# Modulation products and sums of squares issued four at a time, one per column group of TensorE

## The chip, the cores and the metric

The kernel is one program on one core of a Trainium2 chip. The metric is device time in microseconds, the median of several runs of the same program. A core has five engines that run their own instruction streams: TensorE (PE in the profile, with its weight loads shown apart as PEld), VectorE (DVE), ScalarE (ACT), GpSimd (POOL) and SyncE (SP), which issues the DMA transfers. They meet through semaphores.

## The reference

The model is a two-layer backbone for a flow-matching network: 1024 latent tokens with a prefix of 256 context tokens, 1024 features, all in float32. Both layers have the same frame, of which the change touches two parts:

```
def rms_norm(x, g):
    y = x * lax.rsqrt(jnp.mean(x * x, axis=-1, keepdims=True) + EPS)
    return y * g

def ada_mod(cond, w, b):
    m = (silu(cond) @ w + b)          # [1024] @ [1024, 6144]
    return jnp.split(m, 6, axis=-1)   # shift, scale, gate, twice

x = x + gate1 * mixer(rms_norm(x, g1) * (1 + scale1) + shift1)
x = x + gate2 * conv_ffn(rms_norm(x, g2) * (1 + scale2) + shift2)
```

Latent tokens are modulated with the conditioning `c` and context tokens with `c_ctx`. Layer 0's mixer is a gated MLP beside a bidirectional gated DeltaNet; layer 1's mixer is a latent attention of 8 heads. The ConvFFN is a projection up to 5632 features, a depthwise convolution of width 3, `silu(g) * u`, and a projection down. A last RMS norm ends the model.

## The kernel before, in words

Features lie on the 128 partitions, tokens along the free axis. A value of 1024 features is eight tiles `k`, and the tokens are cut into chunks of 256 or 512. Each float32 product of the model's large matrices is made of three float32r passes over halves of the operands (`mm3`, lines 146 to 148: high by high, high by low, low by high), which are 128 columns wide on TensorE. The order of the work on each engine is set by two things: the program's text, in which generators are woven into one another (`weave`, `chain`, `par`: a step of a norm after each step of a product), and then the compiler's scheduler, which moves instructions by its own estimate of when their operands are there.

Two kinds of product are narrow, in full float32, with 32 columns of weights, and their results lie in one of four groups of 32 partitions of a PSUM bank, a column group of TensorE each (`tile_position=(0, 32 * q)`).

*The modulation* (`ada`, line 251). A unit is 512 output features; a layer has 12 units. The weight matrix of a unit comes in four tiles `adaw` of 128 by 1024 elements (512 KB, line 271): tile `k2` holds two `k` tiles of 512 features. When a tile is there, two products are issued (line 281), each over 512 columns, on column groups 0 and 1 or 2 and 3; `start` is set for the first four `k`, `stop` for the last four. After the fourth tile ACT copies the bank to `adam` (line 285), TensorE transposes it in four products (`adat`, line 260) and DVE sums the four groups (line 262). Units 0 to 11 of layer 0 are made before and beside the first mixer's projections; those of layer 1 are made beside layer 0's ConvFFN, one step of the generator after each product group of `up` (`pump`, in `ffn`).

*The norms* (`rnorm`, line 189). For each of the eight tiles a square is made, two of three on ACT (line 203) and one of three on POOL (line 201), and right behind each square comes one product with a matrix of ones (line 205), 256 or 512 columns, on column group `k % 4`. DVE copies the four partial sums (line 208), one more product adds them up and spreads them over the partitions (`nall`, line 211), and DVE and ACT make the reciprocal root (`rsqrt`, line 217). `mod_h` (line 232) then makes the halves `hh`, `hl` of the modulated value with DVE, ACT and POOL. The rooms for squares (`sq`) and for modulated tiles (`h`) are handed out by three functions: `temps` (line 170), `borrow` (line 178) and `carve` (near line 460).

*The places.* Layer 0's second norm is woven between the last products of its output projection (`out0`, tiles `wo`) and the first of the ConvFFN (tiles `up`); the norm before layer 1 runs as a tail beside layer 0's last `down` products (tiles `dn`); layer 1's second norm runs beside the attention's output projection (`out1`); the final norm is the tail of layer 1's ConvFFN, chunk by chunk (`END`), where `ENDP` says after which products the steps of the chunk before are taken. DVE adds each `down` or `wo` result to the stream `xa` (lines 350, 1293, 1605), and DVE and POOL make the halves of every weight tile (lines 132 and 139).

Of the kernel before, what the change touches and what calls it, by code (L numbers as in the profile page):

```python
# [30 lines left out]
# chunks of the tokens (context first), and of the latent ones alone  # L31
CHN = [(0, 256), (256, 512), (768, 512)]
LAT = [(0, 512), (512, 512)]
# the chunks of the first tile and of the last products of a ConvFFN
CHB = [(0, 256), (512, 512), (256, 256), (1024, 256)]
END = [(0, 512), (512, 256), (768, 256)]
# a ConvFFN's order, by its tiles to a group (1 in layer 0, 2 in layer 1): the products after which a step of
# the norm of the chunk before comes, the product from which on the chunk's own norm steps, the steps of the
# last norms within the first tile, and the products held back for the last group
ENDP = {1: (0, 1, 3, 5), 2: (0, 2, 4, 6)}  # L40
# [3 lines left out]
# where the DVE holds the others up: every third sum for the ACT and the Pool  # L44
RELIEF = (3, 1)
# the final norm's tiles for the ACT and the Pool
POOLK = (1, 4, 7)
# GDN: the chunks in rounds of inverses, and the chunks by which the loads of these lag
ROUNDS = [[0, 1, 2, 9], [3, 8, 4, 7], [5, 6]]
LAG = 2  # L50
# gMLP: the chunks from here on stay on the chip
YD = NC - 3
# the queries' tiles: two heads' rotary parts after the first of their plain parts
# [3 lines left out]
def f(ap):  # L57
    return ap.bitcast(F32)


def bc(ap, axis, n):
    """insert a broadcast axis of n at position axis."""
    a = ap.unsqueeze(axis)
    shape = list(a.shape)
    shape[axis] = n
    return a.broadcast_to(shape)
# [8 lines left out]
def weave(main, fill, n=1, rest=True):  # L75
    """n steps of fill after each step of main, then the rest of fill."""
    for _ in main:
        for _ in range(n):
            next(fill, None)
    if rest:  # L80
        drain(fill)


def par(*gens):
    """steps of several generators at once: (generator, steps of it to a step)."""
# [19 lines left out]
class Kern:  # L105
# [4 lines left out]
    # ------------------------------------------------------------ helpers  # L110
    def act(self, out, in_, func, **kw):
        """an activation; Ln and Exp from the table set that has both."""
# [23 lines left out]
    def split(self, hi, lo, src, eng):  # L136
        """src = hi + lo exactly, each in float32r's significand."""
# [3 lines left out]
    def mm3(self, ps, ws, xs, first=True, last=True):  # L141
        """ps += sum of w.T @ x, each product in three float32r passes."""
# [7 lines left out]
    def weights(self, pool, src, shape, tag, eng, bufs_raw=2, bufs=2, n=None):  # L150
        """the halves of a weight (of the first n parts of a room)."""
# [8 lines left out]
    def stream(self, pool, srcs, shape, tag, eng, bufs_raw=2, bufs=2, n=None):  # L160
        """get(i): the halves of the i-th weight; the one after it is to be asked for while it is used."""
# [8 lines left out]
    def temps(self, pool, tag="n", nsq=3, nt=2, nr=2, width=512):  # L170
        """rooms of [P, width] for a norm: called with the temporary's name."""
        def get(name):
            t = {"m": "sq", "t": "sq", "pt": "sq"}.get(name, name)
# [4 lines left out]
    def borrow(self, rooms):  # L178
        """a norm's temporaries in ten rooms."""
        cnt = {"sq": 0, "h": 0}  # L180

        def get(name):
            if name in cnt:
                cnt[name] += 1
                return rooms[4 + cnt[name] % 3 + (3 if name == "h" else 0)]
# [3 lines left out]
    def rnorm(self, tmp, xs, cn, d, res, steps=False):  # L189
        """res: rsqrt(mean over features of x^2 + eps), the same in all partitions, [P, cn].  # L190
        Yields where the PE would wait; with steps, before each x too."""
# [3 lines left out]
        last = {i % g: i for i in range(len(xs))}  # L195
        for i, x in enumerate(xs):
            if steps:
                yield
            sq = tmp("sq")[:, :cn]
            if i % 3 == 2:  # L200
                nc.gpsimd.tensor_tensor(sq, x, x, ALU.mult)
            else:
                nc.scalar.activation(sq, x, AF.Square)
            q = i % g
            nc.tensor.matmul(ps[32 * q:32 * q + 32, :cn], self.ones[:, :32], sq, start=i < g,  # L205
                             stop=i == last[q], tile_position=(0, 32 * q), skip_group_check=True)
# [10 lines left out]
    def rsqrt(self, r, m, t):  # L217
        """r = m ** -0.5: from the tables, then one Newton step.  t is room for a temporary."""
# [7 lines left out]
    def affine(self, t, k, gs, sh, hi, lo):  # L226
        """hi + lo = t * gs + sh (t is overwritten)."""
# [1668 lines left out]
```

## Time and profile before

| what | value |
|---|---|
| median of three runs | 3355.82 us (3353.28 to 3362.9) |
| span of the profiled execution | 3355.8 us |
| PE busy | 3246.5 us (97%), 18141 matmul records |
| DVE, ACT, POOL busy | 60%, 30%, 28% |
| modulation products (line 281), PE busy | 95.2 us, 384 records |
| sums of squares (line 205), PE busy | 91 us, 348 records |

The profile gives no time of the profiled execution beside its span; the span lies within 0.1 us of the median. A full float32 product leaves two records in the trace, a float32r product one, so 384 records are 192 products. [...]

### The profile page before, as it was taken

The page shows a single profiled execution, that of the slowest core. Times are in us where ns is not written, and L with a number is a line of the kernel's source. Part 1 is how long each engine was busy: PE and PEld are TensorE (multiplying, and loading weights), DVE is VectorE, ACT ScalarE, POOL GpSimd, SP SyncE. Part 2 cuts the span into 40 slices and gives each one's busy share as a digit, 9 for nine tenths or more (in the row PEclk, how much of TensorE's full clock was granted, in tenths as well). Part 3 has the DMA queues.
Part 4 walks back from the last instruction along what each step waited for, and adds up shares of the span by engine and source line. Part 5 has one row for each costly group of instructions (what it writes and reads, how often), then busy time and mean ns, then how long its engine had stood idle before and what let it go on. Part 6 is the DMA issues. An engine that isn't in the chain of part 4 may idle for free.

```text
span 3355.8 us, 45952 instructions
## 1 busy us (share of the span) xinstructions
PE 3246.5 (97%) x18141; PEld 2623.7 (78%) x18141; DVE 1998.5 (60%) x3343; ACT 1014.4 (30%) x2116; POOL 943.1 (28%) x993
## 2 busy tenths in 40 slices
PE   7999899999999999999999999999998999999997
PEld 4667777887677877878887778988977788888885
DVE  6333876567666666666665656666656544444445
ACT  5322233333411111111113446555532211111112
POOL 4134323654311111111113332122234322212222
PEclk9999999999999999999999999999999999999999
DMA  7344946752222222221111231000032111111111
GB/s 258 108 132 126 300 137 208 230 154 85 88 70 63 73 72 70 69 76 44 38 38 44 67 102 46 26 22 21 7 132 101 57 44 57 44 44 52 49 38 50
DMA packets 199911, 289.07 MB, mean 86 GB/s; under 512 B 43776, under 2 KB 136400, under 8 KB 199568
## 3 DMA queue, kind: packets, MB, share of 16 engines
q1 hardware_dynamic: 199696, 286.14, 26.9%
q8 instruction: 143, 2.34, 0.3%
q14 instruction: 72, 0.59, 0.1%
HBM read 240.70 MB, written 45.39 MB: 85 GB/s over the span
## 4 chain that ended last, share of the span: by engine, by line
PE 69%; DVE 4%; ACT 2%; issue 1%; POOL 1%; DMA 1%; SPq 0%; DVEq 0%; POOLq 0%; ACTq 0%
PE up L146 11%; PE up L147 11%; PE up L148 11%; PE dn L146 5%; PE dn L147 5%; PE dn L148 5%; PE nsum L205 2%; PE ada L281 1%; PE pt L1532 1%; PE wo L148 1%; PE sc L1501 1%; PE wo L146 1%; PE wo L147 1%; PE o L147 1%; PE o L148 1%
## 5 line engine op out<-in xcount | busy, mean ns | idle before, releaser
L350 DVE SCALAR_TENSOR_TENSOR xa<-dn,mv,xa 128x512 f32<-128x512 f32 (+1 forms) x687 | 438.2, 670 | 402.8 <-PE dn L148 401.6
L132 POOL TENSOR_SCALAR wuh<-wur 128x1024 fp32r<-128x1024 f32 (+1 forms) x134 | 143.1, 1069 | 1108.6 <-PE up L147 1010.4
L365 ACT ACTIVATE raw<-up 128x512 f32<-128x512 f32 (+1 forms) x224 | 123.2, 550 | 1085.7 <-PE up L148 857.0
L146 PE MATMUL up<-hh,wuh 128*128 128x512 f32 (+1 forms) x1072 | 380.4, 356 | 2.1 <-ACT hh L247 1.2
L147 PE MATMUL up<-hl,wuh 128*128 128x512 f32 (+1 forms) x1072 | 377.5, 352 | 0.7 <-POOL hl L230 0.7
L148 PE MATMUL up<-hh,wul 128*128 128x512 f32 (+1 forms) x1072 | 375.9, 351 | 1.2 <-DVE wul L139 1.2
L147 PE MATMUL dn<-al,wdh 128*128 128x512 f32 (+1 forms) x880 | 323.3, 370 | 0.0
L148 PE MATMUL dn<-ah,wdl 128*128 128x512 f32 (+1 forms) x880 | 320.9, 368 | 0.0
L146 PE MATMUL dn<-ah,wdh 128*128 128x512 f32 (+1 forms) x880 | 320.5, 374 | 0.3 <-POOL wdh L132 0.3
L139 DVE TENSOR_TENSOR wul<-wur,wuh 128x1024 fp32r<-128x1024 f32 (+1 forms) x131 | 158.9, 1215 | 197.8 <-POOL wuh L132 197.3
L146 PEld LDWEIGHTS up<-hh,wuh 128*128 128x128 f32 x1072 | 201.9, 189 | 55.9 <-issue 13.4
L147 PEld LDWEIGHTS up<-hl,wuh 128*128 128x128 f32 x1072 | 202.5, 189 | 30.8 <-POOL hl L230 1.1
L148 PEld LDWEIGHTS up<-hh,wul 128*128 128x128 f32 x1072 | 202.4, 189 | 28.9 <-DVE wul L139 1.6
L146 PEld LDWEIGHTS dn<-ah,wdh 128*128 128x128 f32 x880 | 164.1, 189 | 52.6 <-issue 6.4
L148 PEld LDWEIGHTS dn<-ah,wdl 128*128 128x128 f32 x880 | 166.3, 189 | 31.3 <-issue 1.2
L147 PEld LDWEIGHTS dn<-al,wdh 128*128 128x128 f32 x880 | 166.2, 189 | 30.2 <-issue 1.7
L146 PE MATMUL proj<-hh,wih 128*128 128x512 f32 (+1 forms) x512 | 184.7, 362 | 3.4 <-POOL wih L132 3.3
L147 PE MATMUL proj<-hl,wih 128*128 128x512 f32 (+1 forms) x512 | 177.4, 347 | 1.1 <-DVE hl L248 1.1
L480 DVE SCALAR_TENSOR_TENSOR y<-raw,fconv,y 128x1023 f32<-128x1023 f32 (+1 forms) x132 | 161.1, 1221 | 28.1 <-ACT y L366 28.0
L148 PE MATMUL proj<-hh,wil 128*128 128x512 f32 (+1 forms) x512 | 176.9, 346 | 0.0
L1524 POOL TENSOR_SCALAR p<-p,rsm 128x1280 f32<-128x1280 f32 x63 | 84.5, 1341 | 325.8 <-DVE rsm L1517 164.8
L391 POOL TENSOR_TENSOR y<-y,y 128x1280 f32<-128x1280 f32 (+1 forms) x44 | 125.3, 2847 | 168.2 <-DVE y L482 160.5
(451 smaller groups left out, 7813.4 us busy)
## 6 DMA issues: line engine op xcount, KB each, us to landing
adaw<-in_ada_w SPq DMA_DIRECT2D x96, 512.0 KB, 3.6
wur<-in_w_up SPq DMA_DIRECT2D x88, 512.0 KB, 3.5
wdr<-in_w_down SPq DMA_DIRECT2D x44, 512.0 KB, 3.5
t<-t SPq DMA_DIRECT2D x20, 768.0 KB, 6.5
wur<-in_w_out SPq DMA_DIRECT2D x24, 512.0 KB, 3.3
wir<-in_w_t SPq DMA_DIRECT2D x20, 512.0 KB, 4.4
na<-na SPq DMA_DIRECT2D x10, 1024.0 KB, 8.6
t<-kq SPq DMA_DIRECT2D x8, 640.0 KB, 4.2
```

The source lines that it names most:

```text
L132: nc.gpsimd.tensor_scalar(dst, src, 1.0, 0.0, op0=ALU.mult, op1=ALU.add)
L139: (self.nc.gpsimd if eng == "pools" else self.nc.vector).tensor_tensor(lo, src, f(hi), ALU.subtract)
L146: nc.tensor.matmul(ps, wh, xh, start=first and i == 0, stop=False)
L147: nc.tensor.matmul(ps, wh, xl, start=False, stop=False)
L148: nc.tensor.matmul(ps, wl, xh, start=False, stop=last and i == n - 1)
L205: nc.tensor.matmul(ps[32 * q:32 * q + 32, :cn], self.ones[:, :32], sq, start=i < g, stop=i == last[q], tile_position=(0, 32 * q), skip_gro ...
L281: nc.tensor.matmul(ps[32 * q:32 * q + 32, :], self.cst[:, k, :], w[:, 512 * j:512 * j + 512], start=k < 4, stop=k >= 4, tile_position=(0, ...
L350: nc.vector.scalar_tensor_tensor(out=dst, in0=ps, scalar=g2[:, r, ot:ot + 1], in1=dst, op0=ALU.mult, op1=ALU.add)
L365: nc.scalar.activation(raw[:, c0:c0 + cn], ps, AF.Copy)
L391: nc.gpsimd.tensor_tensor(ys[1], ys[0], ys[1], ALU.mult)
L480: nc.vector.scalar_tensor_tensor(out=y[:, s0 + 1:e], in0=raw[:, s0:e - 1], scalar=w[:, 0:1], in1=y[:, s0 + 1:e], op0=ALU.mult, op1=ALU.add)
L1524: nc.gpsimd.tensor_scalar(p, p, rs, 0.0, op0=ALU.mult, op1=ALU.add)
```

## The change

*Modulation.* The weight matrix is laid out anew in memory: tile `k2` now holds four `k` tiles of 256 features each. Each tile thus gives four products of 256 columns, one for each column group, in place of two of 512. The number of tiles, their size and the order of their loads in the program stay. The first two tiles of a unit fill the first 256 columns of the bank, the other two the rest.

*Norms.* `rnorm` collects squares and issues the products of four together, on four column groups, instead of one behind each square. So that four squares can be held, the rooms are divided anew: in `temps` for the norms beside `out0` there are five rooms that squares and modulated tiles share (before, three and two); `borrow` has four for squares instead of three, one shared with `h`; `carve` has four instead of two, with `h` in what is left. `ENDP` for layer 1 is (0, 1, 4, 6) instead of (0, 2, 4, 6). Comments are gone too, so line numbers differ.

```diff
-ENDP = {1: (0, 1, 3, 5), 2: (0, 2, 4, 6)}
+ENDP = {1: (0, 1, 3, 5), 2: (0, 1, 4, 6)}
...
     def temps(self, pool, tag="n", nsq=3, nt=2, nr=2, width=512):
-            t = {"m": "sq", "t": "sq", "pt": "sq"}.get(name, name)
+            t = {"m": "sq", "t": "sq", "pt": "sq", "h": "h" if nt else "sq"}.get(name, name)
...
     def borrow(self, rooms):
-                return rooms[4 + cnt[name] % 3 + (3 if name == "h" else 0)]
+                return rooms[4 + cnt[name] % 4 if name == "sq" else 7 + cnt[name] % 3]
...
     def rnorm(self, tmp, xs, cn, d, res, steps=False):
+        made = []
+        def products():
+            for i, sq in made:
+                q = i % g
+                nc.tensor.matmul(ps[32 * q:32 * q + 32, :cn], self.ones[:, :32], sq, start=i < g,
+                                 stop=i == last[q], tile_position=(0, 32 * q), skip_group_check=True)
+            made.clear()
         for i, x in enumerate(xs):
-            if steps:
+            if steps and i:
                 yield
+            if len(made) == g:
+                products()
             sq = tmp("sq")[:, :cn]
...
-            q = i % g
-            nc.tensor.matmul(ps[32 * q:32 * q + 32, :cn], self.ones[:, :32], sq, start=i < g,
-                             stop=i == last[q], tile_position=(0, 32 * q), skip_group_check=True)
+            made.append((i, sq))
+        if steps:
+            yield
+        products()
...
     def ada(self, pool, tag, l, units, bufs=3, room=None, mp=None):
-                for j in range(2):
-                    k = 2 * k2 + j
-                    q = k % 4
-                    nc.tensor.matmul(ps[32 * q:32 * q + 32, :], self.cst[:, k, :], w[:, 512 * j:512 * j + 512],
-                                     start=k < 4, stop=k >= 4, tile_position=(0, 32 * q), skip_group_check=True)
+                j, kh = divmod(k2, 2)
+                for q in range(4):
+                    nc.tensor.matmul(ps[32 * q:32 * q + 32, 256 * j:256 * j + 256], self.cst[:, 4 * kh + q, :],
+                                     w[:, 256 * q:256 * q + 256], start=kh == 0, stop=kh == 1,
+                                     tile_position=(0, 32 * q), skip_group_check=True)
...
         rooms = self.carve(([f(half_a("ah")), f(half_a("al"))] if G == 1 else [room("raw"), room("raw1")])
-                           + [room("y0"), room("y1")], *([sp.tile([P, 512], F32, tag="dnt", name="dnt")] if G == 1 else []))
+                           + [room("y0"), room("y1")],
+                           sp.tile([P, 512], F32, tag="dnt", name="dnt") if G == 1 else f(half_a("ah"))[:, :512])
...
     def carve(self, rooms, *more):
-        kinds = {"sq": h[0:2], "h": h[2:4] + list(more), **{n: [r] for n, r in zip(("pt", "m", "t", "r"), h[4:])}}
+        kinds = {"sq": h[0:4], "h": list(more) or h[2:4], **{n: [r] for n, r in zip(("pt", "m", "t", "r"), h[4:])}}
+        if more:
+            kinds["h"].append(h[6])
+            kinds["t"] = kinds["pt"]
...
-                tmps = self.temps(np_, nsq=3, nr=1, nt=2, width=256)
+                tmps = self.temps(np_, nsq=5, nr=1, nt=0, width=256)
...
-    o["ada_w"] = i["ada_w"].reshape(2, KD // 2, 2, P, 12, 512).transpose(0, 4, 1, 3, 2, 5).reshape(2, 12, KD // 2, P, 1024)
+    o["ada_w"] = i["ada_w"].reshape(2, 2, 4, P, 12, 2, 256).transpose(0, 4, 5, 1, 3, 2, 6).reshape(2, 12, 4, P, 1024)
```

What the scheduler makes of it is seen in the compiled order of each engine. TensorE's stream holds the same 13104 float32r products before and after, and outside the surroundings of the norms and of the modulation they stand in the same sequence. First, TensorE in layer 0's ConvFFN, where layer 1's modulation lies between the `up` and `dn` products; before:

```order
L147 MATMUL up<-hl_7261,wuh 128x512
L148 MATMUL up<-hh_7260,wul 128x512
L281 MATMUL ada<-adaw,cst_64 32x512 x2
L146 MATMUL dn<-ah,wdh 128x256 x6
L147 MATMUL dn<-al,wdh 128x256
```

and now:

```order
L147 MATMUL up<-hl_7357,wuh 128x512
L148 MATMUL up<-hh_7356,wul 128x512
L292 MATMUL ada<-adaw,cst_64 32x256 x4
L146 MATMUL dn<-ah,wdh 128x256 x6
L147 MATMUL dn<-al,wdh 128x256
```

The place is the same, and four products of 256 columns stand where two of 512 stood. Second, TensorE beside `out0` of layer 0, where a norm of 256 tokens is woven between the `wo` products; before, within one norm:

```order
L148 MATMUL wo<-ybh_7529,wul 128x256
L146 MATMUL wo<-ybh_7529,wuh 128x256
L205 MATMUL nsum<-nsq,cst_66 32x256
L147 MATMUL wo<-ybl_7530,wuh 128x256
L148 MATMUL wo<-ybh_7529,wul 128x256
L146 MATMUL wo<-ybh_7529,wuh 128x256
L147 MATMUL wo<-ybl_7530,wuh 128x256
L148 MATMUL wo<-ybh_7529,wul 128x256
L146 MATMUL wo<-ybh_7529,wuh 128x256
L205 MATMUL nsum<-nsq,cst_66 32x256 x2
```

and now:

```order
L146 MATMUL wo<-ybh_7377,wuh 128x256
L147 MATMUL wo<-ybl_7378,wuh 128x256
L202 MATMUL nsum<-nsq,cst_66 32x256 x4
L146 MATMUL wo<-ybh_7625,wuh 128x256
L147 MATMUL wo<-ybl_7626,wuh 128x256
L202 MATMUL nsum<-nsq,cst_66 32x256
L146 MATMUL wo<-ybh_7377,wuh 128x256
```

The norm's eight products stood in six places and now stand in three: four together, then one, and the last three further on (they are not shown). The scheduler does not keep every four together. Third, DVE at the end of the program, where the final norm of the second of three chunks (512 tokens, then 256 and 256) meets the last sums of `xa`; before:

```order
L213 TENSOR_SCALAR y_27731<-nall 128x256
L350 SCALAR_TENSOR_TENSOR xa_22308<-dn,mv_13316,xa_22308 128x256 x2
L223 SCALAR_TENSOR_TENSOR y_27732<-y_27732,y_27731 128x256
L350 SCALAR_TENSOR_TENSOR xa_22308<-dn,mv_13316,xa_22308 128x256
L224 SCALAR_TENSOR_TENSOR y_27732<-y_27732 128x256
L1805 SCALAR_TENSOR_TENSOR xa_22308<-xa_22308,norm_g,y_27732 128x256 x5
L208 COPY y_27731<-nsum 128x256
```

and now:

```order
L225 TENSOR_SCALAR y_27923<-nall 128x256
L362 SCALAR_TENSOR_TENSOR xa_22500<-dn,mv_13508,xa_22500 128x256
L235 SCALAR_TENSOR_TENSOR y_27923<-y_27923 128x256
L236 SCALAR_TENSOR_TENSOR y_27924<-y_27923,y_27924 128x256
L1820 SCALAR_TENSOR_TENSOR xa_22500<-xa_22500,norm_g,y_27924 128x256 x5
L362 SCALAR_TENSOR_TENSOR xa_22500<-dn,mv_13508,xa_22500 128x256 x2
L220 COPY y_27923<-nsum 128x256
```

The last two sums of `xa` stood ahead of the five products that finish the second chunk and now stand behind them, so that the last chunk's last squares come after these. On SP the number and the sizes of the loads are the same; in the first layer's start the first projection weight `wir` is issued after eleven `adaw` tiles instead of twelve.

More of the change, by code (lines that the diff above doesn't have):

```diff
@@ L445, in ffn @@
         rooms = self.carve(([f(half_a("ah")), f(half_a("al"))] if G == 1 else [room("raw"), room("raw1")])
-                           + [room("y0"), room("y1")], *([sp.tile([P, 512], F32, tag="dnt", name="dnt")] if G == 1 else []))
+                           + [room("y0"), room("y1")], sp.tile([P, 512], F32, tag="dnt", name="dnt") if G == 1 else f(half_a("ah"))[:, :512])
         for c0, cn in ends:
```

## The prediction

> **What bounds the kernel now.** I read the page's busy times and chain first, then stretches of the span by stage, then the narrow products one by one.
>
> ```profile
> PE 3246.5 (97%) x18141; PEld 2623.7 (78%) x18141; DVE 1998.5 (60%) x3343; ACT 1014.4 (30%) x2116; POOL 943.1 (28%) x993
> PE 69%; DVE 4%; ACT 2%; issue 1%; POOL 1%; DMA 1%; SPq 0%; DVEq 0%; POOLq 0%; ACTq 0%
> ```
>
> TensorE is busy for 97% of the span and carries 69% of the chain; the next engine, DVE, carries 4%. By stage (span of the stretch, then PE, PEld, DVE, ACT, POOL busy, clock, DMA share and rate):
>
> ```profile
> 0.00:27.00 27.00, 14.51 (x76) 4.66 (x76) 7.09 (x18) 10.82 (x20) 5.14 (x11) 0.99 0.95 363
> 60.00:270.00 210.00, 200.98 (x1111) 138.39 (x1111) 80.99 (x142) 67.20 (x119) 72.79 (x86) 0.98 0.40 125
> 775.00:880.00 105.00, 101.50 (x575) 72.25 (x576) 77.23 (x136) 45.15 (x104) 40.34 (x54) 1.00 0.28 88
> 880.00:1520.00 640.00, 637.22 (x3246) 507.84 (x3247) 412.48 (x538) 117.13 (x204) 118.52 (x75) 1.00 0.21 69
> 2505.00:2600.00 95.00, 86.00 (x552) 68.17 (x552) 62.48 (x73) 23.96 (x46) 42.47 (x37) 1.00 0.29 101
> 3290.00:3356.00 66.00, 48.69 (x220) 29.41 (x218) 39.91 (x59) 18.84 (x37) 18.55 (x19) 0.91 0.18 64
> ```
>
> From 880 to 1520 us (ConvFFN of layer 0 with layer 1's modulation beside it) TensorE idles 2.8 of 640 us: what leaves its stream there leaves the time. The norms at 775 to 880 and the first projections are nearly as full. The first 27 us are loads (DMA share 0.95), and the last 66 us have TensorE at 74%: chains of the final norm decide there.
>
> **What a narrow product costs the stream.** Four places in the trace (start, duration, records):
>
> ```profile
> 1089.31 0.27 PE L148 MATMUL dn<-ah,wdl 128*128 128x256 f32 x1
> 1089.52 1.05 PE L281 MATMUL ada<-adaw,cst 128*32 128x512 f32 x4
> 1090.50 0.39 PE L146 MATMUL up<-hh,wuh 128*128 128x256 f32 x1
> 1090.72 0.28 PE L147 MATMUL up<-hl,wuh 128*128 128x256 f32 x1
> 1090.84 0.28 PE L148 MATMUL up<-hh,wul 128*128 128x256 f32 x1
> ...
> 813.84 0.28 PE L146 MATMUL wo<-ybh,wuh 128*128 128x256 f32 x1
> 814.04 0.62 PE L205 MATMUL nsum<-nsq,cst 128*32 128x256 f32 x2
> 814.59 0.38 PE L147 MATMUL wo<-ybl,wuh 128*128 128x256 f32 x1
> 814.81 0.28 PE L148 MATMUL wo<-ybh,wul 128*128 128x256 f32 x1
> ...
> 815.50 0.63 PE L205 MATMUL nsum<-nsq,cst 128*32 128x256 f32 x4
> 816.06 0.38 PE L147 MATMUL wo<-ybl,wuh 128*128 128x256 f32 x1
> ...
> 39.42 0.64 PE L205 MATMUL nsum<-nsq,cst 128*32 128x256 f32 x8
> 39.99 0.39 PE L147 MATMUL proj<-hl,wih 128*128 128x256 f32 x1
> ```
>
> Wide products of 256 columns start every 0.12 us (1090.72 to 1090.84). One sum of squares (two records) stretches 813.84 to 814.81 to 0.97 us, where two wide ones alone take 0.24: it costs 0.73. A modulation pair stretches 1089.31 to 1090.72 to 1.41 us: it costs 1.17. So a second 256 columns on the same column group costs 0.43 to 0.44 (a round, below), and about 0.31 is paid once for each place where narrow work breaks into the wide stream, split before and behind: 813.84 to 814.04 is 0.20 instead of 0.12, 814.59 to 814.81 is 0.22. Products on different groups are free beside one another: from the first narrow start to the next wide one it is 0.55 us for one product, 0.56 for two (815.50 to 816.06) and 0.57 for four (39.42 to 39.99). Thus a place costs 0.31 plus 0.43 per round of the fullest column group. A modulation tile goes from 2 rounds to 1; a norm of 256 tokens whose eight products stood alone pays 8 x 0.74 = 5.9 us, and in two fours 1.5.
>
> [...]
>
> **The change part by part.** The compiled order of TensorE gives places and rounds; times are the formula's.
>
> | stage, us | places, rounds before | now | by formula |
> |---|---|---|---|
> | 0 to 27 | 3, 14 | 3, 14 | 0.0 |
> | 27 to 270 | 35, 73 | 38, 52 | -8.1 |
> | 775 to 880 | 30, 38 | 14, 22 | -11.8 |
> | 880 to 1520 | 42, 84 | 42, 42 | -18.0 |
> | 1790 to 1962 | 34, 48 | 32, 45 | -1.9 |
> | 2505 to 2600 | 15, 22 | 11, 17 | -3.4 |
> | 3290 to end | 11, 19 | 14, 20 | +1.3 |
>
> The fours of the norms are not all kept: in layer 1 the scheduler leaves most products of 512 tokens alone, so little is won there. What each term is worth on the path:
>
> ```profile
> 880.00:1520.00 640.00, 44.19 (x168) 6.08 (x168) 1.00 0.21 69
> 800.00:820.00 20.00, 19.63 (x110) 14.61 (x109) 17.74 (x34) 8.51 (x21) 9.45 (x13) 1.00 0.20 52
> PE ada L281 <- DMA adaw<-in_ada_w: 3.2, 2, 1.8
> PE wo L148 <- DVE wul L139: 7.0, 6, 2.3
> PE nsum L205 <- ACT ah L203: 2.1, 5, 0.6
> PE nall L211 <- DVE y L208: 5.0, 2, 3.5
> ```
>
> The first row is the modulation alone: 168 records, two a product and two products a tile, are 42 tiles. 42 x 0.43 = 18.0, and I take all of it, since nothing else is near its limit: DVE is busy 412 of 640 us. From 17.0 to 18.5.
>
> 775 to 880: 11.8, but DVE was busy 17.74 of 20 us at 800 to 820. With the stretch some 2 us shorter it would be full, and its sums of `wo` then hold TensorE's banks; I take 2.5 off: 9.3 (6.5 to 11.8).
>
> 27 to 270: 8.1. TensorE waits 3.2 us here for modulation tiles (two of them, 1.8 the longest); what is won ahead of such a wait is lost at it. I take 7.0 (5.5 to 8.1). The start gains where a unit's last tile lands and its copy, transposes and the first `hh` hang on it: one round, 0.4 (0 to 0.9).
>
> 1790 to 1962: 1.9, and the 2.1 us in which a product waited for a square, because only two rooms rotated, should half go: 3.0 (0 to 4). Here modulated tiles rotate through two rooms instead of three, which is the lower end's reason.
>
> 2505 to 2600: 3.4, but TensorE waits 7.0 us for weight halves (`wul`) that come no sooner; I take 1.5 (0 to 3.4).
>
> The end: +1.3 by formula. Before, the second chunk's sums waited on DVE:
>
> ```profile
> 3328.69 6.91 DVE L1805 SCALAR_TENSOR_TENSOR xa<-xa,norm_g,y 128x512 f32<-128x512 f32 x5
> 3335.52 0.41 DVE L208 COPY y<-nsum 128x256 f32<-128x256 f32 x1
> ```
>
> That copy (and through it `nall`, which waited 5.0 us in all) still stands behind these five. The last chunk's last two sums of `xa` now stand behind the second chunk's five, which adds their 2 x 0.48 us, a square and a product of 0.7 ahead of the last copy; four square rooms take away some 2 us of waits before. I set 0 (-3 to +3).
>
> Sum: 18.0 + 9.3 + 7.0 + 0.4 + 3.0 + 1.5 + 0 = 39.2. The profiled span is 3355.8 and the median of the runs 3355.82, so no offset: **3317 us**. All ends low give 3355.8 - 26 = 3330, all high 3355.8 - 49.7 = 3306.
>
> **Rivals.**
>
> *DVE takes over beside the norms.* TensorE's stream shortens, but where norms are woven in, what feeds it sets the pace (17.74 of 20 us above; 7.0 us for `wul`). Against it: over 775 to 880 DVE has 28 us free. Then only the modulation counts, 18.0 + 7.0 + 0.4: 3330 us.
>
> *More than the stream.* With four square rooms the waits inside the norms go too: the 2.5 us taken off at 775, 2 at 1790, some 4 at the end: 3317 - 8.5 = 3308 us. For it: squares wait for products, not the reverse, where two rooms rotate; against it: the second chunk's copy remains behind DVE's five.
>
> *The groups hold TensorE up: slower.* A four cannot start before its last square, and everything wide queued behind it on TensorE waits too.
>
> ```profile
> 861.58 0.42 ACT L203 ACTIVATE ah<-xa 128x256 f32<-128x256 f32 x1 [1.03 <-PE nsum L205]
> 869.08 0.61 POOL L201 TENSOR_TENSOR ah<-xa 128x256 f32<-128x256 f32 x1 [1.33 <-PE nsum L205]
> 3308.60 0.63 ACT L203 ACTIVATE raw<-xa 128x512 f32<-128x512 f32 x1 [5.16 <-PE nsum L205]
> 3303.28 1.04 POOL L201 TENSOR_TENSOR raw<-xa 128x512 f32<-128x512 f32 x1 [7.12 <-PE nsum L205]
> ```
>
> If it stood through three squares at each of two groups of 15 norms (11 of 256 tokens: 0.42 + 0.42 + 0.61 = 1.45; 4 of 512: 2.3), that is 22 x 1.45 + 8 x 2.3 = 50 us against 39 won: 3367 us. It decides from 1.3 us a group on. Against it: the woven steps put wide products between the squares, and where fours could not be ready the scheduler split them.
>
> *Four streams slow one another.* Each reads its own moving operand, and the trace has but one clean four (0.57 us). If a four cost half a round more, 0.2 us, at some 100 fours: 3317 + 20 = 3337 us. The row itself says 0.02.
>
> [...]
>
> **How the numbers follow.** The forecast 58%, DVE takes over 18%, more than the stream 14%, four streams 5%, slower 3%, and 2% for no effect at all. The likeliest case's own range is 3306 to 3330; with most of its two neighbours 3304 to 3334. Runs of this kernel differ by up to 10 us (3353.28 to 3362.9), so 0.3% is about what can be told from no change. Faster by more than that, below 3345.7, takes in the first four cases: 95%; within it 2%; slower 3%.
>
> **What would show it.** Modulation: 42 places between 880 and 1520 us that cost 0.74 instead of 1.17, the stretch some 18 us shorter, TensorE still above 99% there. Norms: fewer places at 775 to 880 and a stretch near 96 us; if it stays above 99 with DVE above 90%, DVE took over. Fours: a first narrow start to next wide start of 0.57; 0.65 or more means the streams disturb one another. Waits of `nsum` for squares that grow past 10 us would show groups that hold TensorE up. The end: last `xa` sum to end of span. I am wrong if the modulation stretch shrinks by less than 15 us, or if attention and layer 1's ConvFFN, which the order leaves alone, move by more than 3 us each.

## The result, and the profile after

The changed kernel takes **3322.04 us** (median of four runs, 3321.32 to 3323.69) against 3356.61 us for the kernel before beside it: ratio 0.9895, 95% interval 0.9883 to 0.9906. A second set gave 3323.04 us and 0.9896 (0.9883 to 0.9910). The profiled execution's span is 3319.5 us, 36.3 less than before; 39.2 were forecast. The forecast of 3317 us was nearly right as a sum, but one of its terms came out with the wrong sign, and others made up for it. Executions whose granted clock was lower from end to end are left out of the times below; one of them is the profiled execution of the first kernel with weight halves on POOL (0.749 over the span), so its trace gives no times.

First the whole, from the page of the changed kernel: busy times, and the chain that ended last.

```profile
PE 3200.2 (96%) x18525; PEld 2628.9 (79%) x18525; DVE 1996.5 (60%) x3343; ACT 1014.0 (31%) x2116; POOL 947.8 (29%) x993
PE 68%; DVE 4%; ACT 2%; POOL 1%; issue 1%; DMA 0%; DVEq 0%; POOLq 0%; ACTq 0%; SPq 0%
```

PE lost 46 us of busy time, but the span only 36: TensorE idles 10 us more than before. Below, stretches of the span are cut at the same wide products in both kernels, so that each holds the same float32r work. The columns are length, then PE, PEld, DVE, ACT and POOL busy, the granted clock, DMA share and rate. Before:

```profile
0.00:270.08 270.08, 246.22 (x1390) 160.75 (x1391) 112.37 (x204) 99.40 (x196) 95.51 (x120) 0.98 0.50 165
775.21:880.06 104.85, 101.34 (x575) 72.10 (x575) 77.08 (x136) 45.21 (x104) 40.13 (x54) 1.00 0.28 88
880.06:1520.20 640.14, 637.36 (x3247) 507.94 (x3247) 412.42 (x538) 117.07 (x204) 118.52 (x75) 1.00 0.21 69
2505.06:2620.21 115.15, 103.93 (x650) 82.92 (x649) 77.32 (x91) 32.91 (x64) 51.44 (x46) 1.00 0.27 93
```

and after:

```profile
0.00:258.48 258.48, 233.26 (x1583) 163.61 (x1583) 112.20 (x204) 99.86 (x196) 96.51 (x120) 0.97 0.52 173
763.49:871.19 107.70, 94.92 (x601) 74.31 (x599) 76.28 (x135) 43.25 (x102) 43.06 (x54) 0.97 0.28 86
871.19:1494.06 622.87, 620.08 (x3414) 507.97 (x3414) 411.11 (x538) 117.16 (x204) 118.64 (x75) 1.00 0.22 71
2471.55:2585.33 113.78, 101.81 (x650) 84.23 (x649) 76.62 (x91) 31.87 (x63) 52.05 (x45) 0.97 0.28 93
```

The ConvFFN stretch gives 17.3 us and the first 270 give 11.6. The stretch of the norms beside layer 0's output projection (called 775 to 880 below) is the surprise: PE has 6.4 us less to do, and the stretch is 2.9 us longer.

The price of a place, from the timeline of TensorE after: start, duration, records. Records overlap (the one of 0.28 us at 803.38 is followed by a start 0.21 us later), so the price is read from the distance between starts.

```profile
942.20 0.27 PE L148 MATMUL dn<-ah,wdl 128*128 128x256 f32 x1
942.40 0.64 PE L292 MATMUL ada<-adaw,cst 128*32 128x256 f32 x8
942.97 0.39 PE L146 MATMUL up<-hh,wuh 128*128 128x256 f32 x1
943.20 0.28 PE L147 MATMUL up<-hl,wuh 128*128 128x256 f32 x1
...
802.59 0.64 PE L202 MATMUL nsum<-nsq,cst 128*32 128x256 f32 x8
803.16 0.39 PE L146 MATMUL wo<-ybh,wuh 128*128 128x256 f32 x1
803.38 0.28 PE L147 MATMUL wo<-ybl,wuh 128*128 128x256 f32 x1
803.59 0.62 PE L202 MATMUL nsum<-nsq,cst 128*32 128x256 f32 x2
804.14 0.39 PE L146 MATMUL wo<-ybh,wuh 128*128 128x256 f32 x1
```

From 942.20 to 943.20 it is 1.00 us where two wide products alone take 0.24, so a modulation tile now costs 0.76, against 1.17 before; 42 tiles at 0.41 are 17.2, and the stretch gave 17.3. A four takes 0.57 us from its first start to the next wide one (942.40 to 942.97, 802.59 to 803.16), a single product 0.55 (803.59 to 804.14): four column groups really run beside one another.

What ate the gain of the norms is seen in the waits of TensorE (waited for, us in total, times, longest). Before, 775.21 to 880.06, the first rows:

```profile
PE up L146 <- ACT hh L247: 1.2, 1, 1.2
PE wo L148 <- DVE wol L139: 0.7, 1, 0.7
PE nall L211 <- DVE npt L208: 0.7, 1, 0.7
```

After, 763.49 to 871.19:

```profile
PE nsum L202 <- ACT nsq L214: 3.9, 1, 3.9
PE wo L147 <- DVE ybl L139: 1.8, 1, 1.8
PE nsum L202 <- POOL nsq L212: 1.8, 1, 1.8
PE up L146 <- ACT hh L259: 1.7, 2, 1.2
```

and the longest of them, in the timeline of the changed kernel (the brackets: idle before, and what ended it):

```profile
822.44 0.47 DVE L260 SCALAR_TENSOR_TENSOR hl<-nh,mv,hh 128x256 fp32r<-128x256 f32 x1
822.94 0.42 ACT L214 ACTIVATE nsq<-xa 128x256 f32<-128x256 f32 x1 [2.62 <-DVE hl L260]
823.41 1.06 PE L202 MATMUL nsum<-nsq,cst 128*32 128x256 f32 x2 [3.92 <-ACT nsq L214]
```

The square of the next norm begins only when DVE has made `hl` of the norm before, because that step frees one of the five shared rooms; the sum waits for the square, and the wide `wo` products queued behind the sum wait with it.

For all kernels below, the stretch 775 to 880 splits into three parts: the time in which TensorE idles (gaps between its instructions), half of the time at half clock (the most that the half clock can lose), and the rest, called stream. "Places" are counted in the trace, with those of the full float32 sums `nall` and `on`, so they are a few more than in the prediction. Each row is one profiled execution; the two of the changed kernel differ by 2.8 us.

| kernel | length | places | idle | half-clock loss | stream |
|---|---|---|---|---|---|
| before | 104.9 | 33 | 3.5 | 0 | 101.3 |
| after | 107.7 | 17 | 12.8 | 3.4 | 91.5 |
| after, again | 110.5 | 17 | 13.0 | 6.8 | 90.7 |
| rooms apart | 102.1 | 19 | 9.2 | 1.7 | 91.1 |
| alone, rooms of before | 103.9 | 30 | 6.5 | 0 | 97.4 |
| alone, shared rooms | 116.1 | 26 | 12.9 | 10.2 | 92.9 |
| modulation only | 103.3 | 31 | 4.1 | 0 | 99.2 |
| norms only | 110.1 | 17 | 11.7 | 6.8 | 91.6 |
| twos, rooms of before | 102.4 | 26 | 7.5 | 0 | 94.9 |
| rooms apart, copy on ACT | 103.0 | 18 | 9.3 | 1.7 | 92.0 |
| rooms apart, copy on ACT, later | 98.2 | 17 | 8.5 | 0 | 89.7 |
| rooms apart, later | 102.8 | 18 | 10.1 | 3.4 | 89.3 |
| twos, weight halves on POOL | 103.9 | 28 | 5.8 | 0 | 98.1 |

The two kernels called later hold fewer modulation products in this stretch. The stream shrinks with the places as forecast (101.3 to 91.5 with the change); idle time and half clock grow with it by 12.7 us. The other stretches follow further below.

### The profile page after: what moved, and what is told of

Its sections match the earlier page's. It is cut to its first block, busy times and chain, and to the rows that moved or that the text cites. A ratio compares the mean times of both kernels' runs of the same rounds, so it can differ in the third digit from the quotient of the medians.

```text
span 3319.5 us, 46730 instructions
## 1 busy us (share of the span) xinstructions
PE 3200.2 (96%) x18525; PEld 2628.9 (79%) x18525; DVE 1996.5 (60%) x3343; ACT 1014.0 (31%) x2116; POOL 947.8 (29%) x993
## 4 chain that ended last, share of the span: by engine, by line
PE 68%; DVE 4%; ACT 2%; POOL 1%; issue 1%; DMA 0%; DVEq 0%; POOLq 0%; ACTq 0%; SPq 0%
PE up L146 11%; PE up L147 11%; PE up L148 11%; PE dn L146 5%; PE dn L147 5%; PE dn L148 5%; PE nsum L202 1%; PE pt L1547 1%; PE sc L1516 1%; PE wo L148 1%; PE wo L146 1%; PE wo L147 1%; PE o L147 1%; PE o L148 1%; PE o L146 1%
```

## The experiments

**The change again**, unedited, beside the three kernels that follow, to see how far its stretches scatter.

> The changed kernel once more, as the yardstick for the three beside it: span 3319 to 3322 us. In the changed kernel's first trace the stretch with layer 0's second norm (from the wide product that starts at 775.2 us before to the one that starts at 880.1) took 107.7 us instead of 104.9, though its narrow products should cost 11.8 us less; TensorE stood 15.9 us there instead of 6.2, the longest time 3.9 us for a square.

Measured: 3323.04 us (3320.93 to 3324.56), profiled span 3322.8, with 775 to 880 at 110.5 and 880 to 1520 at 622.9. The long wait for a square is in both profiles.

**Rooms apart.** Theory A: the shared rooms make squares wait for modulated tiles. Theory B: a group of four waits for its last square, whatever the rooms. Theory C: DVE sets the pace. The edit gives the modulated tiles four rooms of their own, in a part of `yb` that is no longer needed:

```diff
-                tmps = self.temps(np_, nsq=5, nr=1, nt=0, width=256)
+                base, yr, cnt = self.temps(np_, nsq=5, nr=1, nt=0, width=256), [yb[:, j, 0:256] for j in range(4)], [0]
+                def tmps(name):
+                    if name != "h":
+                        return base(name)
+                    cnt[0] += 1
+                    return yr[cnt[0] % 4]
```

> The changed kernel, but the norms beside layer 0's output projection keep their modulated tiles in four rooms of their own (a part of yb that is no longer needed) instead of sharing the squares' five. Theory A (shared rooms: the next norm's squares wait until the last norm's modulated tiles are used up, and TensorE stands at the product behind them): the 3.9 us wait is gone, the stretch takes 97 to 100 us, the whole 8 to 11 us less than the changed kernel, 3309 to 3314. Theory B (a group of four waits for its last square, whatever the rooms): the stretch stays within 2 us of 107.7 and the whole within 3 us. Theory C (DVE sets the pace there): the same as B, with DVE above 90% of the stretch.

Measured: 3318.81 us (3314.8 to 3319.74), ratio 0.9882 (0.9868 to 0.9895), stretch 102.1. The wait for the square is gone, but a new one stands 3.4 us at the sum over the partitions:

```profile
828.68 2.54 DVE L258 SCALAR_TENSOR_TENSOR o<-xa,gs,nr 128x256 f32<-128x256 f32 x3
831.14 0.86 DVE L1308 SCALAR_TENSOR_TENSOR xa<-wo,mv,xa 128x256 f32<-128x256 f32 x2
831.93 0.41 DVE L220 COPY npt<-nsum 128x256 f32<-128x256 f32 x1
832.39 1.22 PE L223 MATMUL nall<-npt,cst 128*128 128x256 f32 x2 [3.37 <-DVE npt L220]
```

The copy of the four sums stands behind modulated tiles and `wo` sums on DVE. Theory A has the direction, but the stretch falls by 5.6 us (8.4 against the second profile), not to 97 to 100; B, with a stretch within 2 us of 107.7, falls.

**Alone, with the rooms of before, and alone, with shared rooms.** Both issue each sum by itself in these norms; they differ only in the rooms, since the second keeps the five shared ones (`nsq=5`, `nt=0`).

```diff
-            if len(made) == g:
+            if len(made) == (1 if getattr(tmp, "alone", False) else g):
...
-                tmps = self.temps(np_, nsq=5, nr=1, nt=0, width=256)
+                tmps = self.temps(np_, nsq=3, nr=1, nt=2, width=256)
+                tmps.alone = True
```

> The changed kernel, but in the norms beside layer 0's output projection each square's product is issued alone, with the old division of rooms (three and two). Theories A and B: the stretch as before the change, 104 to 106 us, the whole 2 to 4 us less than the changed kernel. Theory C: 107 to 108 us, as in the changed kernel.

> The changed kernel with its five shared rooms, but in these norms each square's product is issued alone. Theory A: TensorE still waits for squares that have no room; the stretch stays at 107 us or more, the whole within 3 us of the changed kernel. Theory B: the waits go, the stretch takes 105 us or less, the whole 3 to 5 us less than the changed kernel.

Measured: 3319.0 us (ratio 0.9886, 0.9871 to 0.9902), stretch 103.9, with the rooms of before; 3326.12 us (0.9904, 0.9888 to 0.9919), stretch 116.1, with shared rooms. The latter's waits:

```profile
PE nsum L202 <- ACT nsq L214: 7.8, 2, 6.9
```

and the longer one in its timeline:

```profile
828.43 1.06 PE L202 MATMUL nsum<-nsq,cst 128*32 128x256 f32 x2 [6.88 <-ACT nsq L214]
```

So the shared rooms bring the waits without any group of four. In the profiled executions they cost 12.2 us in this stretch: 6.4 more of idle time and 10.2 of half clock, less 4.5 of stream. That size is not sure, since the profiled execution with shared rooms took 3333.18 us, the longest of its four; in the medians the two kernels are 7.1 us apart, and the intervals of their ratios overlap. The direction is theory A's, and C (107 to 108 for the kernel with the rooms of before) falls.

**The two halves of the change apart.** Modulation only is the kernel before with the new layout and the new product loop; norms only is the changed kernel with the old ones.

```diff
-                for j in range(2):
-                    k = 2 * k2 + j
-                    q = k % 4
-                    nc.tensor.matmul(ps[32 * q:32 * q + 32, :], self.cst[:, k, :], w[:, 512 * j:512 * j + 512], ...)
+                j, kh = divmod(k2, 2)
+                for q in range(4):
+                    nc.tensor.matmul(ps[32 * q:32 * q + 32, 256 * j:256 * j + 256], self.cst[:, 4 * kh + q, :],
+                                     w[:, 256 * q:256 * q + 256], ...)
...
-    o["ada_w"] = i["ada_w"].reshape(2, KD // 2, 2, P, 12, 512).transpose(0, 4, 1, 3, 2, 5).reshape(2, 12, KD // 2, P, 1024)
+    o["ada_w"] = i["ada_w"].reshape(2, 2, 4, P, 12, 2, 256).transpose(0, 4, 5, 1, 3, 2, 6).reshape(2, 12, 4, P, 1024)
```

> The kernel before with the modulation's change alone (the weight's layout and four products of 256 columns a tile); the norms are as before. If the terms of the sum stand apart, the whole gain of the ConvFFN stretch is here (880 to 1520 us at 622 to 624), and that of the first 270 us (258 to 262), which was 8.1 by the formula and about 11.5 measured; 775 to 880 stays at 103.5 to 106 and the whole comes 26 to 31 us under the kernel before. If the norms' fours had a share in the first stretch, its gain here stays under 9 us and the whole under 26.

> The changed kernel with the modulation as before; the norms' fours, their rooms and the order at the end stay. If the terms stand apart: 880 to 1520 at 640, the first 270 us at 268 to 270, 775 to 880 at 107 to 112 (slower than before, 104.9), 1790 to 1962 at 167, 2505 to 2620 and the end 1 to 2 us less; the whole 4 to 10 us under the kernel before. If the norms' part were worth what the sum gave it (9.3 + 3.0 + 1.5 and a share of the first stretch), the whole would be 14 us under or more.

Measured: modulation only 3325.88 us (3321.66 to 3330.19), ratio 0.9900 (0.9886 to 0.9914); norms only 3355.07 us (3347.63 to 3358.99), ratio 0.9985 (0.9976 to 0.9995). The kernel before beside them had 3359.25. The three rows are 0 to 270, 775 to 880 and 880 to 1520 with modulation only,

```profile
0.00:259.07 259.07, 234.87 (x1582) 164.88 (x1583) 112.32 (x204) 100.08 (x196) 97.97 (x120) 0.97 0.52 172
762.65:865.99 103.34, 99.22 (x600) 72.73 (x599) 75.45 (x136) 44.74 (x104) 40.74 (x54) 1.00 0.28 90
865.99:1488.88 622.89, 620.49 (x3415) 509.19 (x3414) 411.16 (x538) 117.14 (x204) 118.57 (x75) 1.00 0.22 71
```

and with norms only:

```profile
0.00:268.60 268.60, 244.70 (x1390) 160.21 (x1391) 112.39 (x204) 99.33 (x196) 95.67 (x120) 0.99 0.50 166
772.21:882.35 110.14, 98.40 (x575) 75.48 (x575) 76.67 (x136) 42.70 (x100) 43.53 (x54) 0.94 0.27 84
882.35:1523.03 640.68, 637.43 (x3246) 508.01 (x3246) 412.34 (x538) 117.81 (x206) 118.65 (x75) 1.00 0.21 69
```

The terms stand apart as expected, with small misses: 775 to 880 came out at 103.3 with modulation only where 103.5 to 106 were expected, and 2505 to 2620 at 111.8 with norms only, 3.4 us under the kernel before instead of 1 to 2. Modulation only came 2 us beyond its expected range for the whole (33.4 against 26 to 31 under the kernel before): the two stretches from 270 to 775, where TensorE's products stay the same, range from 250.1 to 255.4 and from 251.0 to 254.6 over the profiles, so 2 us lie within their scatter. In the medians the modulation is worth about 33 us and the norms by themselves about 4 to 5. Both together are worth 34.6, and the ratios 0.9900 with modulation only and 0.9895 with the whole change have overlapping intervals, so that the norms add anything to the modulation is not shown. Norms only, at 110.1 in its stretch, loses there 5.3 us of what it wins in layer 1 and at the end.

**The copy on ACT.** On top of rooms apart, the four partial sums of these norms are copied by ACT.

```diff
-        nc.vector.tensor_copy(part[:32 * g, :cn], ps[:32 * g, :cn])
+        if getattr(tmp, "onact", False):
+            nc.scalar.copy(part[:32 * g, :cn], ps[:32 * g, :cn])
+        else:
+            nc.vector.tensor_copy(part[:32 * g, :cn], ps[:32 * g, :cn])
...
+                tmps.onact = True
```

> The kernel with the modulated tiles in rooms of their own, and the copy of the four partial sums on ACT instead of DVE for the norms beside the output projection. With the rooms apart TensorE's longest stand was 3.4 us at the sum over the partitions, behind DVE's copy, which stood behind three products of modulated tiles on DVE. If DVE's queue is what is late next, the stretch 775 to 880 goes from 102.1 to 97 to 100 and the whole to 3313 to 3317. If ACT's queue (squares of the next norm, halves of weights) holds the copy as long, the stretch stays at 101 to 104 and the whole within 2 us of the kernel with rooms apart.

Measured: 3321.05 us (3315.25 to 3321.99), ratio 0.9883 (0.9868 to 0.9899), stretch 103.0. The stretch lies where the second theory put it, but neither theory is right: the wait for the copy is gone, and TensorE now stands at a modulation product for its tile, which it reached sooner than the load.

```profile
PE ada L295 <- DMA adaw<-in_ada_w: 3.4, 1, 3.4
PE wo L148 <- DVE wul L139: 2.1, 2, 1.1
```

**Twos.** The changed kernel with groups of two and the rooms of before.

```diff
-            if len(made) == g:
+            if len(made) == (2 if getattr(tmp, "alone", False) else g):
...
-                tmps = self.temps(np_, nsq=5, nr=1, nt=0, width=256)
+                tmps = self.temps(np_, nsq=3, nr=1, nt=2, width=256)
+                tmps.alone = True
```

> The changed kernel, but the norms beside the output projection issue two products at a time and have the rooms of before (three for squares, two for modulated tiles). If only the shared rooms were at fault, pairs win over single products what they save in places (26 places and 51 rounds in the compiled stretch where single products have 30 and 55, by the formula 3.0 us): 775 to 880 at 100 to 102.5 against 103.9 with single products. If a group's wait for its last square eats what its place saves, the stretch is at 103.5 to 106.

Measured: 3320.03 us (3313.35 to 3322.88), ratio 0.9877 (0.9861 to 0.9894), stretch 102.4, at the upper end of what shared rooms alone would make it. Against single products the stream gained 2.5 us and the idle time grew by 1.0; the 1.5 us that are left are less than the 2.8 us between two profiles of one kernel.

**Later.** On top of the copy on ACT, layer 1's modulation begins eight steps later; the second kernel does the same with the copy on DVE.

```diff
             def ada1():
+                for _ in range(8):
+                    yield
                 yield from self.ada(ffw, "wur", 1, range(12))
```

> The kernel with rooms apart and the partial sums copied on ACT, and layer 1's modulation begun eight steps later in the ConvFFN, so that its first tiles are not asked for beside the norms. In the kernel without that last edit TensorE stood 3.4 us at a modulation product for its tile, and one half-clock slice of 3.4 us followed. If the tile's load is what is late next there, that wait and the slice go: 775 to 1520 us, 726.0 in the kernel without it, comes to 720 to 723 (the products move, they are not saved) and the whole to 3309 to 3315 in the profiled execution's terms, 3 to 5 us under it. If the norms' chain or DVE sets this stretch whatever TensorE does, another wait takes its place and 775 to 1520 stays at 724.5 to 727.

> The same, but the partial sums are copied on DVE as in the changed kernel: rooms apart and the modulation begun eight steps later. If DVE's queue holds the copy, TensorE stands some 3.4 us at the sum over the partitions as it did with rooms apart, with a half-clock slice behind it: 775 to 1520 at 723.5 to 726, 2.5 to 4 us more than with the copy on ACT. If the copy's engine does not matter, the two are within 1.5 us.

Measured: 3317.53 us (3316.93 to 3318.09), ratio 0.9877 (0.9863 to 0.9891), and 3321.88 us (3321.57 to 3325.37), ratio 0.9894 (0.9880 to 0.9909). With the copy on ACT, 775 to 1520 us takes 722.4 as expected, 3.5 less than without the delay. But the next stretch, which holds the end of the modulation now, takes 273.4 instead of 269.9, so the sum is the same (995.8 and 995.9), the whole did not come out 3 to 5 us shorter as expected (3315.3 us of span in the profiled execution against 3313.5), and other waits stand in the place of the load:

```profile
PE nall L226 <- ACT npt L221: 2.2, 1, 2.2
PE wo L148 <- DVE wul L139: 2.1, 2, 1.1
PE up L146 <- ACT hh L262: 1.3, 2, 1.0
```

With the copy on DVE the wait for it is back (3.8 us), and 775 to 1520 takes 726.2, 3.8 more: that part of the theory holds.

**Weight halves on POOL.** Is it DVE's load that sets this stretch? The low halves of the output projection's weights go to POOL, in the kernel with rooms apart and in that with twos.

```diff
-                get = self.stream(ffw, w_half1 * 2, [P, KD, P], "wu", "pool", 3, n=4)
+                get = self.stream(ffw, w_half1 * 2, [P, KD, P], "wu", "pools", 3, n=4)
```

> The kernel with modulated tiles in rooms of their own, and the low halves of the output projection's weights (14 subtractions of 0.69 us beside the norms) made on POOL instead of DVE: some 10 us of 75 leave DVE's queue in the stretch 775 to 880 and some 12 go to POOL's 42. If DVE's queue is what holds TensorE there, the stand of 3.4 us at the sum over the partitions falls under 1.5, and the stretch goes from 102.1 to 97 to 100, the whole to 3312 to 3316 in the profiled execution. If the stretch is set by the chain of the norm across the engines, or POOL becomes late for the weights, it stays at 101.5 to 106 and other waits take the place.

> The same move of the weights' low halves to POOL in the kernel that issues two products at a time with the rooms of before (102.4 us in the stretch 775 to 880, with TensorE idle 7.5). If DVE's queue holds TensorE: 98 to 100.5, idle under 5. If not: 102 to 106.

Measured: 3331.93 us, ratio 0.9915 (0.9901 to 0.9929), for the first, and 3320.2 us, ratio 0.9894 (0.9880 to 0.9908), stretch 103.9, for the second. The first is slower than rooms apart without the edit (0.9882, 0.9868 to 0.9895); where, its trace cannot say. In the second TensorE idles less (5.8 us against 7.5), but it has 28 places instead of 26 and a stream of 98.1 us instead of 94.9: the compiled order changed too, so this is no clean test. The idle time did not fall under 5 us, and the stretch did not get shorter. That DVE's load by itself sets the stretch is thus not borne out, but not excluded either.

## Why the prediction was right, and where it was not

Gains in us by stretch. The split is in stream, idle and half-clock loss as above, minus for what was won. In the first row the split begins at the thirteenth wide product (31.9 us before, 33.7 after), in the last it ends at the last wide product.

| stretch | forecast | measured | stream | idle | half clock |
|---|---|---|---|---|---|
| start and 27 to 270 | 7.4 | 11.6 | -11.3 | -1.0 | -1.2 |
| 775 to 880 | 9.3 | -2.9 | -9.8 | +9.3 | +3.4 |
| 880 to 1520 | 18.0 | 17.3 | -17.2 | 0 | 0 |
| 1790 to 1962 | 3.0 | 4.7 | -3.6 | +0.6 | -1.7 |
| 1962 to 2505 | 0 | 2.6 | -0.6 | -2.1 | 0 |
| 2505 to 2620 | 1.5 | 1.4 | -5.5 | +0.8 | +3.4 |
| from 3290 | 0 | 1.4 | -2.4 | +0.7 | +0.8 |

*The modulation in the ConvFFN* was right: forecast 18.0, measured 17.3, with a place at 0.76 where the formula said 0.74. TensorE stays above 99% busy.

*Fours are free beside one another* was right: 0.57 us for a four against 0.55 for one product, and the rival "four streams slow one another" would have needed 0.65 or more.

*775 to 880* is the step that failed: "I take 2.5 off: 9.3 (6.5 to 11.8)". It came out 2.9 us slower. The formula for places was right, since the stream gave 9.8 us of its 11.8. What the step did not see is that a stretch can lose its slack in other ways than on DVE. Two causes are seen. The five rooms that squares and modulated tiles share make the squares of one norm wait for the modulated tiles of the norm before (a stretch 5.6 to 8.4 us shorter with rooms apart, and 12.2 us between the profiles of the two kernels with single products). And the half clock follows long waits (last section), 3.4 us here and 6.8 in the second profile. The rival "the groups hold TensorE up" had the right victim, wide products queued behind a sum that waits for its square, but as its cause the group itself and as its price 1.45 or 2.3 us at each of 30 groups. In the trace there is one stand of 3.9 and one of 1.8, and the cause is the rooms; products issued alone suffer as well (7.8). Over the whole program the waits of `nsum` for squares grew from 4.9 to 9.3 us, just short of the 10 that were to be this rival's sign.

With this cause removed the stretch still takes 102.1 to 103.9 us in five variants, 0.9 to 2.8 less than before, and 103.3 with the modulation alone; the kernel before was profiled once, so a gain of this size is not clear of the scatter. (The 98.2 and 102.8 of the kernels called later come with modulation products moved out.) Each time a wait went, the next one stood in its place: the copy of the sums on DVE, then a modulation tile's load, then that copy on ACT and weight halves. Which of them is the floor is open. The rival "DVE takes over" was thus right in that little but the modulation counts. Its sign was half there: the stretch stayed above 99 us, but DVE was busy for 76.3 of 107.7 us, 71% and not 90%. It also took the first stretch too small, so that its 3330 us was not reached.

*27 to 270* was mis-sized: 8.1 by the formula, 7.0 taken, 11.3 in the stream. Modulation only has the whole of it (a stream of 223.5 us before and 211.5 with modulation only). By the distance from each narrow product's start to the next start, modulation products went from 31.8 to 26.5 us and the sums of squares `l` of the first mixer from 13.2 to 8.0. In the changed kernel these lie between modulation products and run beside them:

```profile
138.25 0.85 PE L292 MATMUL ada<-adaw,cst 128*32 128x256 f32 x11
138.72 0.59 PE L778 MATMUL l<-sq,cst 128*32 128x512 f32 x1
138.92 0.61 PE L292 MATMUL ada<-adaw,cst 128*32 128x256 f32 x6
139.15 0.59 PE L778 MATMUL l<-sq,cst 128*32 128x512 f32 x1
```

This second part is what the step left out. The start itself, up to 31.9 us, lost 1.8 us where 0.4 were to be won.

*1790 to 1962*: 4.7 against 3.0 (0 to 4), beyond its bounds. The 2.1 us of waits for squares went whole, where half was taken, but other waits came and the idle time grew by 0.6; the gain is 3.6 of stream and 1.7 of half clock. *2505 to 2620*: 1.4 against 1.5, which is luck, since it came for another reason: the stream gave 5.5, and half-clock slices took 3.4 back (norms only, without such slices, takes 111.8 us here against 113.8), while the wait for `wul` stayed:

```profile
PE wo L148 <- DVE wul L139: 7.4, 6, 2.5
```

*The end*: 1.4 against 0 (-3 to +3), inside its bounds.

That the sum came out only 2.9 us off is thus in part luck. The 12.2 us missing at 775 to 880 were made up by 4.2 in the first stretch, 1.7 at 1790 to 1962, 1.4 at the end, and 2.6 in a stretch that the change leaves alone. In the medians the gain is 34.6 us of the 39.2. "No offset" was not right either: in every run that lists both, the time is 1.8 us above the span.

What was to prove the whole wrong did not come: layer 1's ConvFFN, 2620 to 3290, takes 669.9 us in every profile but the one at 0.749, and attention moved by less than 3. *1962 to 2505*, which holds it, moved by 2.6 us, and in both halves of the change as well (539.7 and 539.9 against 542.9). TensorE's instructions there are the same; the kernel before was profiled once and had 2.1 us more idle time. In one other profile of a changed kernel the stretch took 543.0, so this is read as scatter of that stretch and not as an effect.

No version is shown to beat the change. The best ratios (0.9877 for twos and for the later start) lie below 0.9895, but their intervals overlap its interval. What can be said from the stretches is that rooms apart, twos or single products with the rooms of before each take 4 to 6 us less than the change's first profile at 775 to 880.

## What to carry to other kernels

When products on different column groups can be issued together, price the places and rounds (here 0.31 us a place and 0.43 a round of 256 columns); where the stream really is the bound, as in the ConvFFN, that price arrives (17.3 us of 18.0 there). Where several engines pass a chain to one another, work removed from the fullest engine can return as waiting, as it did beside the norms (9.8 us less of stream, 9.3 more of idle time): before counting on the gain, list which waits were just hidden and follow the rooms, because a buffer pool merged to save space ties the start of one step to the end of another. A wait on TensorE has to be priced with the half-clock slice that can follow it, as one followed all 148 of this case's slices with more than 2.1 us idle.

## What the hardware did that was not expected

The granted clock of TensorE falls to one half in slices of 3.4 us, and it does so after idle time shorter than a slice (2.31 us in the second case below). In the changed kernel, consecutive slices (length, then PE, PEld, DVE, ACT, POOL busy, and the clock):

```profile
816.30:819.70 3.40, 3.19 (x27) 2.98 (x25) 3.40 (x6) 1.89 (x4) 3.12 (x5) 1.00 0.34 137
819.70:823.10 3.40, 0.00 (x0) 0.00 (x0) 3.40 (x7) 0.78 (x3) 3.32 (x4) 1.00 0.55 154
823.20:826.60 3.40, 3.19 (x12) 2.38 (x13) 3.26 (x5) 1.88 (x6) 1.12 (x2) 0.50 0.12 25
826.60:830.00 3.40, 3.36 (x40) 2.44 (x39) 2.19 (x5) 2.18 (x8) 1.51 (x2) 1.00 0.34 129
830.00:833.40 3.40, 1.09 (x9) 0.58 (x9) 1.62 (x2) 0.19 (x1) 1.67 (x2) 1.00 0.83 289
833.40:836.80 3.40, 3.40 (x18) 3.33 (x17) 1.45 (x4) 1.25 (x3) 0.07 (x1) 0.50 0.47 178
```

The slice without any PE work (819.70) is followed by one at 0.50, in which 12 records run instead of 27 or 40. The slice with 2.31 us idle (830.00) is followed by one too. All half-clock stretches of a profile begin on one grid of 3.41 us, within 0.01. Over thirteen profiles (all but the one at 0.749), the slices of that grid sort by TensorE's idle time in them, without those ahead of a profile's first clock record (9.5 us into the span before, 10.8 after):

| idle in the slice, us | next slice at full clock | at half clock |
|---|---|---|
| under 0.3 | 11490 | 13 |
| 0.3 to 0.9 | 538 | 16 |
| 0.9 to 1.5 | 240 | 39 |
| 1.5 to 2.1 | 57 | 72 |
| over 2.1 | 0 | 148 |

In a slice that is itself at half clock, less idle time was enough: of those with 0.9 to 1.5 us idle, 27 of 27 were followed by another at half clock, against 12 of 252 where the slice itself had the full clock.

So a stand of about 2 us can cost up to 1.7 us more behind it, half of a slice of 3.4 us: 72 of the 129 slices with 1.5 to 2.1 us idle were followed by one at half clock, and all 148 with more. The whole of the change has 79.7 us at half clock against 59.3 before: up to 10.2 us of its gain went that way.
